# A hybrid attention block: second copies of queries and keys taken from SBUF, a changed input order, and a later first division

## The chip, the cores and the metric

The kernel runs on one core of one Trainium2 chip. The metric is the device time in microseconds of that core, from three runs of the kernel before; a separate profiled execution gives the profile.

## The reference

One decoder block over 1024 positions of width 1024, in float32. The part that matters here, cut:

```python
u = rms_norm(h, norm_mix)
proj = u @ w_in                      # S5 input, q, k, v, forget logits, gates
y_ssm = gelu(s5_ssm(...));  out_a = glu(y_ssm @ w_glu)
log_f = log_sigmoid(f_logit); cum = cumsum(log_f)
s = (q @ k.T) * 64**-0.5 + cum[t] - cum[s]       # 8 heads of 64, causal
att = softmax(s) @ v
h = h + (gate_a * out_a + gate_b * (att @ w_fox_o)) @ w_mix_out
h = h + memory_cross_attention(...)  # 256 memory tokens, 4 heads of 128, keys and values = rms_norm(mem) @ w_mem_kv
h = h + swiglu_ffn(rms_norm(h));  out = rms_norm(h)
```

## The kernel before

A float32 product is made of three matmuls of a rounded high part and a low part each (`mm3`, lines 173 to 175: high·high, high·low, low·high). A `split` makes the two parts: a cast on ScalarE (ACT, line 183) and a subtraction on VectorE (DVE, line 184). Nearly all of the time TensorE (PE) multiplies; ACT and DVE evacuate PSUM and make high and low parts; POOL (GpSimd) makes a few low parts; SP issues the DMAs.

The stages in time: input (0 to about 60 us: memory tokens and input are normalised and transposed, the keys and values of the memory and the S5 input are projected), gates and S5 (to 300), values of the forgetting attention (to 366), its eight heads (to 560), GLU and mixing (to 740), memory attention (to 920), feed-forward (to 1538).

A scheduler places each engine's instructions by the order in which the program emits them, by their dependences and by its own cost estimates. An engine executes its instructions in that order, and each waits for its semaphores. `B.behind(x)` places what is emitted in it no earlier than behind instruction `x`.

**Input.** `stage_in` emits the steps that the table `ORDER_IN` (line 41) lists. `K0` to `K3` are the projections of the four memory heads' keys (24 matmuls of 128x256 each; the weights `whi`, `wlo` of a head are split by `W0` to `W3`, `k` evacuates), `Tn0`, `Em0` and the like transpose and evacuate halves of a memory tile, `T00` to `T71` and `E..` the same for the tiles `xt` of the input (line 237 the transposes, into the PSUM banks `misc` and `pv`; lines 183 and 184 the evacuations `uh`, `ul`), `Q` the squares for the norm, `D` and `F` loads, `V` the memory's values (banks `sc`, evacuated into `kv`), `U..` the projection of the S5 input (`mm`).

**A head.** `project(h)` returns the steps of head h's queries and keys: `load`, `split` of the weights, 16 `parts` (each one contraction tile of one half of 512 positions) into a PSUM bank `mm` of three, and two `evac`. An `evac` writes four tiles `hb` (K1, K2, Q1, Q2, two sets, used by heads in turn): ACT writes the high parts to the rows 0 to 63 of Q1 and K1 (lines 1725, 1726), DVE the low parts to one half of Q2 and K2 (1727, 1729), and ACT writes the high parts a second time to the other half (1732, 1733). Scores then take two matmuls (1793 with the gates' rows and the maxima's row, 1794 with Q2 and K2).

A head has 12 units (a query half and a key tile). For each: `scores` (two matmuls into a bank `sc` of two, on the diagonal a DVE addition of the mask, line 1796; the exponential `pf` on ACT, 1800; its high part `ph` on ACT, 1805, or for four of the units on DVE, 1802; its low part `pl` on DVE, 1806, or for those four units on POOL, 1803), and one or two units later the products with the values (1818, 1819, 1825). Between the units, `run` emits what is listed in `side[i]`: row maxima of the next head (1763 on PE into `mm`, 1765 and 1768 on DVE), `parts`, `evac` and weight splits of the head after it. `max_row` turns the maxima into a row and sends it by DMA (1781). At the end of a head `finish` makes reciprocals through DRAM (`rb`), and in the next head `divide` multiplies by them (1846, DVE, 64x1024) and splits the result (`ahi`, `alo`).

Of the kernel before, what the change touches and what calls it, by code (L numbers as in the profile page):

```python
# [13 lines left out]
AF = mybir.ActivationFunctionType  # L14
# [24 lines left out]
RSLOT_LATE = (0, 1, 2, 3, 4, 4, 5, 5, 6, 6, 7, 7)  # L39

ORDER_IN = """
Fm G0 Fn G1 D0 X10 B0 b0 Qm Qn Rm D1 Sm F1 B1 Tm0 Tm1 b1 Rn Sn Tn0 F0 D2 Em0 Tn1 En0 W0 Em1 En1 D3 F2 F3 W1 C1 Q0 Q1 K0 D4 F4 F5 K1 R0
S0 T00 T01 k0 E00 Q2 W2 D5 F6 F7 E01 S1 T10 Q3 W3 k1 K3 K2 W4 E10 W5 D6 R1 k2 T11 k3 S2 Q4 V0 S3 T30
E11 D7 D8 D9 Da Q5 T20 R2 T21 E21 E20 S4 E30 W6 Db y0 L0 W7 T40 V1 S5 E40 T31 V2 E31 W8 T41 V3 E41 W9 T50 Q6 v T51 E51
U00 Q7 R3 S6g u00 L1 T60 E50 S7g Wa T61 T70 E61 Wb U10 E60 T71 E70 E71 P0 y1 U20 u10 u20 P1 U21 U11 U30
P2 u30 U31 u11 u31 U01 u21 P3 P4 P5 u01
# [20 lines left out]
def f32(ap):  # L67
    return ap.bitcast(F32)
# [1503 lines left out]
            self.B.S.dma_start(y_d[q, i].rearrange("t (m g) c -> (t m) g c", g=8), f32(y).rearrange("p (g c) -> p g c", g=8))  # L1572


Projection = namedtuple("Projection", "load split parts evac")


class Fox:
# [111 lines left out]
    def project(self, h):  # L1690

        B = self.B
        V, A, S = B.V, B.A, B.S
        K1, K2, Q1, Q2 = self.hb[h % 2]

        def load(behind=None):
            src = lambda c: self.w_in[:, c + h * DH:c + (h + 1) * DH].rearrange("(k p) c -> p k c", p=P)
            raw = self.raw[h] = B.wpool.tile([P, RAW], F32, tag="raw", bufs=4, name="raw")[:, :D]
            rv = raw.rearrange("p (k c) -> p k c", k=8)
            with B.behind(behind):  # L1700
                S.dma_start(rv[:, :, 0:64], src(C_Q))
                return S.dma_start(rv[:, :, 64:128], src(C_K))

        def parted(behind=None):
            wh = B.wpool.tile([P, WSLOT], F32R, tag="whi", name="whi")[:, :D]
            wl = B.wpool.tile([P, WSLOT], F32R, tag="wlo", name="wlo")[:, :D]
            with B.behind(behind):
                cast = B.split(wh, wl, self.raw.pop(h))
            self.pj[h] = [t.rearrange("p (k c) -> p k c", k=8) for t in (wh, wl)]
            return cast  # L1710

        def part(hf, k):
            if k == 0:
                self.pj[h, hf] = B.bank("mm")
            wh, wl = self.pj[h]
            rh, rl = self.uT.rhs(k, hf)
            with B.behind(self.maxed if h == 1 else None):
                self.parted = B.mm3(self.pj[h, hf], wh[:, k, :], wl[:, k, :], rh, rl, k == 0, k == 7)

        def evac(hf, between=None):  # L1720
            if hf == 1 and h > 1:
                self.gate_rows(h)
            ps = self.pj.pop((h, hf))
            cs = slice(512 * hf, 512 * hf + 512)
            A.activation(Q1[0:64, cs], ps[0:64, :], AF.Copy, scale=0.125)
            copied = A.copy(K1[0:64, cs], ps[64:128, :])
            V.scalar_tensor_tensor(out=Q2[64:128, cs], in0=ps[0:64, :], scalar=0.125, in1=f32(Q1[0:64, cs]),
                                   op0=ALU.mult, op1=ALU.subtract)
            V.tensor_sub(K2[0:64, cs], ps[64:128, :], f32(K1[0:64, cs]))
            cast = between(copied) if between else None  # L1730
            with B.behind(cast):
                A.activation(Q2[0:64, cs], ps[0:64, :], AF.Copy, scale=0.125)
                A.copy(K2[64:128, cs], ps[64:128, :])
            return cast

        return Projection(load, parted, [lambda hf=hf, k=k: part(hf, k) for hf in range(2) for k in range(8)],
                          [lambda: evac(0), lambda between=None: evac(1, between)])

    def gate_rows(self, h):
        K1, K2, Q1, Q2 = self.hb[h % 2]  # L1740
# [118 lines left out]
    def run(self, y_d, yT, aT, w_glu, w_d, filler):  # L1859
        B, fp, S = self.B, self.fp, self.B.S  # L1860
        self.aT = aT
        self.prepare_v()
        for t in range(NT):
            self.values_of_v(1, t)
        self.log_forget()
        self.setup()

        def load_y(k, h):

            with B.behind(self.maxima[NH - 2] if h else self.spread[NH - 4]):  # L1870
# [22 lines left out]
        for f in pro[0].parts[:8] + pro[0].evac[:1] + pro[0].parts[8:] + pro[0].evac[1:]:  # L1893
# [12 lines left out]
        with B.behind(self.negated):  # L1906
            ready = pro[1].evac[1](pro[2].split)
        self.values_of_v(0, 4)
        pro[3].load()
        self.values_of_v(0, 5, ready)  # L1910
        with B.behind(turned):
            self.values_of_v(0, 6, ready)
        units = [(qc, kt) for qc in range(2) for kt in range(4 * qc + 4)]
        for h in range(NH):
            side = {i: [] for i in range(12)}
            late = h == NH - 2
            if late:
                for i, f in enumerate(pro[h + 1].parts[8:]):
                    side[i // 2].append(f)
                side[3].append(pro[h + 1].evac[1])  # L1920
            if h + 1 < NH:
                for i, f in enumerate(self.row_max(h + 1)):
                    side[(RSLOT_LATE if late else RSLOT)[i]].append(f)
                side[9].append(lambda: self.max_row(h + 1))
            if h + 2 < NH:
                n = 8 if h + 3 == NH else 16
                for i, f in enumerate(pro[h + 2].parts[:n]):
                    side[i if n == 8 else PSLOT[i]].append(f)
                side[9].append(pro[h + 2].evac[0])
                if n == 16:  # L1930
                    side[11].append(pro[h + 2].evac[1])
            if h + 3 < NH:
                side[9].append(lambda: pro[h + 3].split(self.exp))
            for n_ in {1: (4, 5), 2: (6,), 3: (7,)}.get(h, ()):
                side[5].append(lambda n_=n_: pro[n_].load(self.spread[h - 1]))
            if h == 0:
                side[0].append(lambda: self.values_of_v(0, 7))
            if late:
                for k in range(8):
                    side[4 + k].append(lambda k=k: load_y(k % 4, k // 4))  # L1940
            if h == NH - 1:
                for k in range(3):
                    side[6 + k].append(lambda k=k: load_att(k))
                for i, f in enumerate(filler):
                    side[i * 12 // len(filler)].append(lambda i=i, f=f: first_glu(i, f))
            for i, u in enumerate(units):
                self.scores(h, *u)
                for f in side[i]:
                    f()
                if len(self.hi_todo) > 2:  # L1950
                    self.values_hi()
                if len(self.lo_todo) > 1:
                    self.values_lo()
                if h and i == 5:
                    with B.behind(self.left):
                        self.divide(h - 1)
        while self.hi_todo:
            self.values_hi()
        while self.lo_todo:
            self.values_lo()  # L1960
        self.divide(NH - 1)
# [29 lines left out]
```

## Time and profile before

| | us |
|---|---|
| median of three runs (1538.91, 1540.33, 1540.62) | 1540.33 |
| the profiled execution | 1539.77 |
| its span, first to last instruction | 1538.1 |
| PE busy in it | 1520.7 |
| DVE busy | 1005.7 |
| ACT busy | 658.1 |
| POOL busy | 253.6 |
| PE busy in 400 to 420 us | 18.76 of 20 |
| PE busy in 920 to 1520 us | 600.00 of 600 |

PE's clock was granted at 0.999 throughout. PE is busy for 99% of the span, so the other engines' busy time decides only where PE waits for them; the idle time of PE, 17.4 us, lies in a few places.

### The profile page before, as it was taken

The page shows a single profiled execution, that of the slowest core. Times are in us where ns is not written, and L with a number is a line of the kernel's source. Part 1 is how long each engine was busy: PE and PEld are TensorE (multiplying, and loading weights), DVE is VectorE, ACT ScalarE, POOL GpSimd, SP SyncE. Part 2 cuts the span into 40 slices and gives each one's busy share as a digit, 9 for nine tenths or more (in the row PEclk, how much of TensorE's full clock was granted, in tenths as well). Part 3 has the DMA queues.
Part 4 walks back from the last instruction along what each step waited for, and adds up shares of the span by engine and source line. Part 5 has one row for each costly group of instructions (what it writes and reads, how often), then busy time and mean ns, then how long its engine had stood idle before and what let it go on. Part 6 is the DMA issues. An engine that isn't in the chain of part 4 may idle for free. (4 is left out here: it accounts for less than half of the span.)

```text
span 1538.1 us, 20434 instructions
## 1 busy us (share of the span) xinstructions
PE 1520.7 (99%) x7329; PEld 1257.7 (82%) x7329; DVE 1005.7 (65%) x1828; ACT 658.1 (43%) x1183; POOL 253.6 (16%) x341
## 2 busy tenths in 40 slices
PE   8999999999999999999999999999999999999998
PEld 7888888898777678888888888888888888888886
DVE  7936554355878867675556797777777775675555
ACT  7423334324667643232435663333333333354343
POOL 1166542100121214100102200000000000101001
PEclk9999999999999999999999999999999999999999
DMA  9634556611223746378210356555544544896542
GB/s 286 161 104 102 131 128 144 180 41 16 50 46 88 192 131 198 111 218 308 89 69 1 117 204 210 162 161 160 158 158 157 157 145 139 291 391 220 192 163 110
DMA packets 196293, 234.06 MB, mean 152 GB/s; under 512 B 35576, under 2 KB 127656, under 8 KB 195680
## 3 DMA queue, kind: packets, MB, share of 16 engines
q1 hardware_dynamic: 188704, 214.93, 47.0%
q10 hardware_dynamic: 7488, 17.83, 3.1%
q8 instruction: 57, 0.93, 0.3%
q14 instruction: 44, 0.36, 0.1%
HBM read 161.94 MB, written 72.71 MB: 153 GB/s over the span
## 5 line engine op out<-in xcount | busy, mean ns | idle before, releaser
L184 DVE TENSOR_TENSOR wlo<-raw,whi 128x1024 fp32r<-128x1024 f32 (+2 forms) x120 | 126.3, 1058 | 45.4 <-ACT whi L183 44.2
L183 ACT CAST whi<-raw 128x1024 fp32r<-128x1024 f32 (+2 forms) x120 | 108.7, 910 | 105.6 <-PE mm L174 39.1
L184 DVE TENSOR_TENSOR ol<-or,oh 128x1024 fp32r<-128x1024 f32 x73 | 90.1, 1236 | 74.0 <-ACT oh L183 71.9
L173 PE MATMUL mm<-uh,whi 128*128 128x512 f32 x344 | 136.5, 397 | 0.0
L174 PE MATMUL mm<-ul,whi 128*128 128x512 f32 x344 | 135.1, 393 | 0.0
L175 PE MATMUL mm<-uh,wlo 128*128 128x512 f32 x344 | 134.5, 391 | 0.0
L183 ACT CAST oh<-or 128x1024 fp32r<-128x1024 f32 x73 | 76.9, 1054 | 105.0 <-PE mm L1108 34.2
L997 POOL TENSOR_TENSOR g<-a,c 128x512 f32<-128x512 f32 x22 | 35.7, 1621 | 389.0 <-ACT a L996 389.0
L175 PEld LDWEIGHTS mm<-uh,wlo 128*128 128x128 f32 x344 | 64.7, 188 | 13.3 <-DVE wlo L184 0.2
L1803 POOL TENSOR_TENSOR pl<-pf,ph 128x512 fp32r<-128x512 f32 (+1 forms) x32 | 36.8, 1152 | 232.5 <-DVE ph L1802 193.3
L173 PEld LDWEIGHTS mm<-uh,whi 128*128 128x128 f32 x344 | 64.8, 188 | 11.6
L174 PEld LDWEIGHTS mm<-ul,whi 128*128 128x128 f32 x344 | 64.8, 188 | 11.0
L1800 ACT ACTIVATE pf<-sc 128x512 f32<-128x512 f32 (+1 forms) x96 | 46.4, 489 | 44.5 <-DVE sc L1796 28.3
L986 DVE SCALAR_TENSOR_TENSOR c<-c,pv 128x512 f32<-128x512 f32 x22 | 15.1, 687 | 76.5 <-ACT c L985 76.4
L211 POOL TENSOR_TENSOR r<-ms,mhalf 128x1 f32<-128x1 f32 (+1 forms) x26 | 15.7, 605 | 298.6 <-DVE ms L207 258.5
L964 PE MATMUL pv<-S3h,we 128*128 128x512 f32 x176 | 57.7, 389 | 0.0
L1806 DVE TENSOR_TENSOR pl<-pf,ph 128x512 fp32r<-128x512 f32 (+2 forms) x64 | 35.3, 553 | 10.4 <-ACT ph L1805 9.8
L1108 PE MATMUL mm<-ol,oh 128*128 128x512 f32 (+1 forms) x110 | 41.9, 381 | 0.0
L1108 PE MATMUL mm<-oh,ol 128*128 128x512 f32 (+1 forms) x110 | 41.9, 381 | 0.0
L1108 PE MATMUL mm<-oh 128*128 128x512 f32 (+1 forms) x110 | 41.9, 381 | 0.0
L173 PE MATMUL sc<-uh,whi 128*128 128x512 f32 x104 | 40.8, 392 | 0.0
L173 PE MATMUL mm<-yh,whi 128*128 128x512 f32 x104 | 40.7, 392 | 0.0
(639 smaller groups left out, 4554.2 us busy)
## 6 DMA issues: line engine op xcount, KB each, us to landing
or<-c_d SPq DMA_DIRECT2D x77, 256.0 KB
wo<-in_w_ffn_out_dram SPq DMA_DIRECT2D x22, 512.0 KB
c_d<-g SPq DMA_DIRECT2D x44, 256.0 KB
t_d<-wo SPq DMA_DIRECT2D x44, 256.0 KB
or<-t_d SPq DMA_DIRECT2D x44, 256.0 KB
rawb<-in_w_ffn_in_dram SPq DMA_DIRECT2D x20, 512.0 KB
raw<-in_w_ffn_in_dram SPq DMA_DIRECT2D x20, 512.0 KB
raw<-in_w_in_dram SPq DMA_DIRECT2D x19, 512.0 KB
```

The lines of the kernel that those rows point to most:

```text
L173: T.matmul(ps, lh, rh, start=first, stop=False)
L174: T.matmul(ps, lh, rl, start=False, stop=False)
L175: return T.matmul(ps, ll, rh, start=False, stop=last)
L183: cast = self.A.copy(hi, src)
L184: self.rest = (self.G if pool_lo else self.V).tensor_sub(lo, src, f32(hi))
L211: self.G.tensor_tensor(out=r, in0=v, in1=self.mhalf[:, 0:n], op=ALU.pow)
L964: T.matmul(ps, l_[:, k, :], r_, start=first and k == 0 and i == 0, stop=k == 3 and i == 2, skip_group_check=True)
L997: G.tensor_mul(g[:, 512:], a1, c1)
L1108: T.matmul(ps, l_[:, gi], r_[:, c0:c1], start=k == 0 and (p == NP - LAST if own else p == 0 and n in (1, 2, 7)), stop=p == NP - 1 and k == ...
L1800: self.exp = A.activation(pf[:, off:], ps[:, off:], AF.Exp)
L1803: G.tensor_sub(pl[:, off:], pf[:, off:], f32(ph[:, off:]))
L1806: self.left = V.tensor_sub(pl[:, off:], pf[:, off:], f32(ph[:, off:]))
```

## The change

It has four parts.

1. The second copies leave `evac`. A new step `double` of a projection makes them from the SBUF tiles Q1 and K1 instead of PSUM. They stand behind an exponential in the head that comes just before: half 0 in `side[4]` and half 1 in `side[8]` of head h − 1; head 0's own follow its `evac` steps.
2. Between the first head's row maxima and its scores, the split of head 2's weights stood in the midst of head 1's `evac(1)`; it now follows it.
3. The first `divide`, of head 0 in head 1, stands behind unit 7 instead of 5. The other heads keep 5.
4. In `ORDER_IN`, `Em1` comes directly behind `Em0`, and `K2` ahead of `K3`.

```diff
-...Tn0 F0 D2 Em0 Tn1 En0 W0 Em1 En1 D3 ...
+...Tn0 F0 D2 Em0 Em1 Tn1 En0 W0 En1 D3 ...
-...W3 k1 K3 K2 W4...
+...W3 k1 K2 K3 W4...

-        def evac(hf, between=None):
+        def evac(hf):
...
-            cast = between(copied) if between else None
-            with B.behind(cast):
-                A.activation(Q2[0:64, cs], ps[0:64, :], AF.Copy, scale=0.125)
-                A.copy(K2[64:128, cs], ps[64:128, :])
-            return cast
+            return copied
+
+        def double(hf):
+            cs = slice(512 * hf, 512 * hf + 512)
+            with B.behind(self.exp if h else None):
+                A.copy(Q2[0:64, cs], f32(Q1[0:64, cs]))
+                A.copy(K2[64:128, cs], f32(K1[0:64, cs]))
...
-            ready = pro[1].evac[1](pro[2].split)
+            copied = pro[1].evac[1]()
+        ready = pro[2].split(copied)
...
+                side[4].append(pro[h + 1].double[0])
+                side[8].append(pro[h + 1].double[1])
...
-                if h and i == 5:
+                if h and i == (7 if h == 1 else 5):
```

Lines of the changed kernel are three higher than before from 1735 on (four in `run`'s start, six in its loop).

**The order on PE in the input**, around 20 us. The names: `mm_272` is the bank of the second head's keys, `mm_355` and `mm_380` those of the next two; `whi_328` and `wlo_329` are the third head's weights, `whi_349` the fourth's; `misc_306` and `pv_311` are transposes of an input tile. Before:

```order
L175 MATMUL mm_272<-mh1_0_111,wlo_233 128x256
L173 MATMUL mm_355<-mh0_0_110,whi_349 128x256
L174 MATMUL mm_355<-ml0_0_112,whi_349 128x256
L237 MATMUL misc_306<-ident_69,xt_205 128x128 x4
L237 MATMUL pv_311<-ident_69,xt_205 128x128 x4
L173 MATMUL mm_380<-mh0_0_110,whi_328 128x256
L174 MATMUL mm_380<-ml0_0_112,whi_328 128x256
```

Now:

```order
L173 MATMUL mm_355<-mh0_0_110,whi_328 128x256
L174 MATMUL mm_355<-ml0_0_112,whi_328 128x256
L175 MATMUL mm_355<-mh0_0_110,wlo_329 128x256
L173 MATMUL mm_355<-mh0_0_110,whi_328 128x256
L174 MATMUL mm_355<-ml0_0_112,whi_328 128x256
L175 MATMUL mm_355<-mh0_0_110,wlo_329 128x256
L173 MATMUL mm_355<-mh0_0_110,whi_328 128x256
L174 MATMUL mm_355<-ml0_0_112,whi_328 128x256
L175 MATMUL mm_355<-mh0_0_110,wlo_329 128x256
L173 MATMUL mm_355<-mh0_0_110,whi_328 128x256
L174 MATMUL mm_355<-ml0_0_112,whi_328 128x256
L237 MATMUL misc_306<-ident_69,xt_205 128x128 x4
```

The third head's matmuls now come before the fourth's, and eleven of them stand ahead of the transposes in place of two.

**The order on DVE in the input**, around 41 to 44 us, where the S5 input's first matmuls read `ul0` (the low half of a transposed input tile, `ul0_0_95`) and `wlo_578`; `kv` are the memory's values. Before:

```order
L184 TENSOR_TENSOR ul0_0_95<-misc_472,uh0_0_87 128x2x128
L209 TENSOR_SCALAR ms2_652<-ss2_611 128x2
L184 TENSOR_TENSOR ul3_0_101<-pv_556,uh3_0_93 128x2x128
L215 TENSOR_TENSOR rt2_654<-r02_653 128x2
L216 SCALAR_TENSOR_TENSOR rt2_654<-rt2_654,ms2_652 128x2
L217 SCALAR_TENSOR_TENSOR r02_653<-rt2_654,r02_653 128x2
L184 TENSOR_TENSOR wlo_578<-xw_465,whi_577 128x1024
L184 TENSOR_TENSOR ul1_0_97<-misc_472,uh1_0_89 128x2x128
L184 TENSOR_TENSOR kv_319<-sc_439,kv_318 128x512
```

Now:

```order
L184 TENSOR_TENSOR kv_319<-sc_439,kv_318 128x512
L184 TENSOR_TENSOR ul3_0_101<-pv_556,uh3_0_93 128x2x128
L215 TENSOR_TENSOR rt2_654<-r02_653 128x2
L216 SCALAR_TENSOR_TENSOR rt2_654<-rt2_654,ms2_652 128x2
L184 TENSOR_TENSOR wlo_578<-xw_465,whi_577 128x1024
L184 TENSOR_TENSOR ul0_0_95<-misc_472,uh0_0_87 128x2x128
L184 TENSOR_TENSOR kv_319<-sc_446,kv_318 128x512
L184 TENSOR_TENSOR ul1_0_97<-misc_472,uh1_0_89 128x2x128
```

`ul0` moved from ahead of `wlo_578` to behind it, and one eviction `kv` to ahead of it.

**The order on DVE in head 1**, around 408 to 416 us, where `num<-num,rb` is the division's multiply and `alo` its low part. Before:

```order
L1802 CAST ph<-pf 128x512
L1846 TENSOR_TENSOR num<-num,rb 64x1024
L1768 TENSOR_REDUCE mc<-mm 128x1
L1727 SCALAR_TENSOR_TENSOR hb_3274<-mm,hb_3273 64x512
L184 TENSOR_TENSOR alo<-num,ahi 64x1024
L1806 TENSOR_TENSOR pl<-pf,ph 128x512
L1765 ISA junk,mc<-mm,tri 128x384
```

Now:

```order
L1805 CAST ph<-pf 128x512
L1771 TENSOR_REDUCE mc<-mm 128x1
L1727 SCALAR_TENSOR_TENSOR hb_3274<-mm,hb_3273 64x512
L1809 TENSOR_TENSOR pl<-pf,ph 128x512
L1768 ISA junk,mc<-mm,tri 128x384
L1768 ISA mc 128x1
L1849 TENSOR_TENSOR num<-num,rb 64x1024
L1799 TENSOR_TENSOR sc<-sc,trk 128x128
L1771 TENSOR_REDUCE mc<-mm 128x1
L1799 TENSOR_TENSOR sc<-sc,trk 128x128
L184 TENSOR_TENSOR alo<-num,ahi 64x1024
L1805 CAST ph<-pf 128x512
```

The multiply moved behind a row maximum, a low part of head 2's projection, a subtraction and another maximum; the low part `alo` now stands ahead of a `ph` cast.

More of the change, by code (lines that the diff above doesn't have):

```diff
@@ L41 @@
 ORDER_IN = """
-Fm G0 Fn G1 D0 X10 B0 b0 Qm Qn Rm D1 Sm F1 B1 Tm0 Tm1 b1 Rn Sn Tn0 F0 D2 Em0 Tn1 En0 W0 Em1 En1 D3 F2 F3 W1 C1 Q0 Q1 K0 D4 F4 F5 K1 R0
-S0 T00 T01 k0 E00 Q2 W2 D5 F6 F7 E01 S1 T10 Q3 W3 k1 K3 K2 W4 E10 W5 D6 R1 k2 T11 k3 S2 Q4 V0 S3 T30
+Fm G0 Fn G1 D0 X10 B0 b0 Qm Qn Rm D1 Sm F1 B1 Tm0 Tm1 b1 Rn Sn Tn0 F0 D2 Em0 Em1 Tn1 En0 W0 En1 D3 F2 F3 W1 C1 Q0 Q1 K0 D4 F4 F5 K1 R0
+S0 T00 T01 k0 E00 Q2 W2 D5 F6 F7 E01 S1 T10 Q3 W3 k1 K2 K3 W4 E10 W5 D6 R1 k2 T11 k3 S2 Q4 V0 S3 T30
 E11 D7 D8 D9 Da Q5 T20 R2 T21 E21 E20 S4 E30 W6 Db y0 L0 W7 T40 V1 S5 E40 T31 V2 E31 W8 T41 V3 E41 W9 T50 Q6 v T51 E51
@@ L1572, in store @@
             self.B.S.dma_start(y_d[q, i].rearrange("t (m g) c -> (t m) g c", g=8), f32(y).rearrange("p (g c) -> p g c", g=8))
-Projection = namedtuple("Projection", "load split parts evac")
+Projection = namedtuple("Projection", "load split parts evac double")
 class Fox:
@@ L1729, in evac @@
             V.tensor_sub(K2[0:64, cs], ps[64:128, :], f32(K1[0:64, cs]))
-            cast = between(copied) if between else None
-            with B.behind(cast):
-                A.activation(Q2[0:64, cs], ps[0:64, :], AF.Copy, scale=0.125)
-                A.copy(K2[64:128, cs], ps[64:128, :])
-            return cast
+            return copied
[4 more added lines that the diff above has]
+                A.copy(K2[64:128, cs], f32(K1[0:64, cs]))
         return Projection(load, parted, [lambda hf=hf, k=k: part(hf, k) for hf in range(2) for k in range(8)],
-                          [lambda: evac(0), lambda between=None: evac(1, between)])
+                          [lambda: evac(0), lambda: evac(1)],
+                          [lambda: double(0), lambda: double(1)])
     def gate_rows(self, h):
@@ L1892, in run @@
                             w_glu[k * P:(k + 1) * P].rearrange("(g m) c -> m g c", m=16))
-        for f in pro[0].parts[:8] + pro[0].evac[:1] + pro[0].parts[8:] + pro[0].evac[1:]:
+        for f in pro[0].parts[:8] + pro[0].evac[:1] + pro[0].parts[8:] + pro[0].evac[1:] + pro[0].double:
             f()
```

## The prediction

> **What bounds the kernel now.** I read the busy shares first, then the busy time by stretch, then what TensorE waited for, and last the timeline around each of those waits.
>
> The head of the page:
>
> ```profile
> span 1538.1 us, 20434 instructions
> ...
> PE 1520.7 (99%) x7329; PEld 1257.7 (82%) x7329; DVE 1005.7 (65%) x1828; ACT 658.1 (43%) x1183; POOL 253.6 (16%) x341
> ```
>
> TensorE (PE) is idle for 1538.1 − 1520.7 = 17.4 us in all. The change adds and removes no matmul, so only some of those 17.4 us can be won. Where they lie shows in the busy time by stretch (start:end, length, then busy us of PE, PEld, DVE, ACT, POOL with instruction counts in brackets, clock, DMA share, GB/s):
>
> ```profile
> 20.00:40.00 20.00, 18.65 (x121) 16.11 (x121) 19.25 (x38) 15.51 (x33) 1.70 (x3) 1.00 0.93 236
> 400.00:420.00 20.00, 18.76 (x91) 14.06 (x91) 16.92 (x39) 11.99 (x22) 4.60 (x4) 1.00 0.50 94
> 920.00:1520.00 600.00, 600.00 (x2647) 496.41 (x2646) 399.10 (x533) 233.05 (x336) 45.43 (x30) 1.00 0.57 187
> ```
>
> The feed-forward part is full, and the change can do nothing there. What it can reach are the 1.35 us that PE is idle in 20 to 40, and holes like the 1.24 us of 400 to 420 in the attention heads. PE's waits with their causes (engine and line waited for: us in total, times, longest):
>
> ```profile
> PE mm L1763 <- DVE mc L1768: 1.2, 1, 1.2
> PE mm L173 <- ACT whi L183: 1.1, 1, 1.1
> PE misc L237 <- DVE xt L231: 1.1, 2, 0.9
> PE sc L1793 <- ACT pf L1800: 0.7, 2, 0.5
> PE pv L1818 <- DVE ph L1802: 0.5, 1, 0.5
> PE mm L1763 <- DVE mc L1765: 0.3, 1, 0.3
> PE pv L1818 <- ACT ph L1805: 0.3, 1, 0.3
> PE mm L1763 <- ACT hb L1733: 0.3, 1, 0.3
> ```
>
> The whole that the change could win if every one of these went is 1.2 + 1.1 + 1.1 + 0.7 + 0.5 + 3 × 0.3 = 5.5 us, or 0.36% of the time. That is the ceiling. The question is how much of it stays won, because PE stands in a chain with DVE and ACT, and a stall that goes lets PE run into the next late buffer.
>
> **The start (K2 ahead of K3, Em1 early).** These are the rows around 17 to 23 us (start, length, engine, line, what, and in brackets the idle time before with its releaser):
>
> ```profile
> 17.16 1.07 ACT L183 CAST whi<-raw 128x1024 fp32r<-128x1024 f32 x1
> 18.07 0.28 PE L175 MATMUL mm<-mh,wlo 128*128 128x256 f32 x1
> 18.19 0.28 PE L173 MATMUL mm<-mh,whi 128*128 128x256 f32 x1
> 18.27 1.23 DVE L184 TENSOR_TENSOR wlo<-raw,whi 128x1024 fp32r<-128x1024 f32 x1 [0.72 <-ACT whi L183]
> 20.46 1.07 ACT L183 CAST whi<-raw 128x1024 fp32r<-128x1024 f32 x1
> 20.98 2.48 DVE L231 SCALAR_TENSOR_TENSOR xt<-xt,r,gain 128x1024 f32<-128x1024 f32 x2
> 21.58 0.39 PE L173 MATMUL mm<-mh,whi 128*128 128x256 f32 x1 [1.11 <-ACT whi L183]
> 22.32 0.66 PE L237 MATMUL misc<-ident,xt 128*128 128x128 f32 x4 [0.23 <-DVE xt L231]
> ```
>
> The cast at 17.16 is that of the third head's key weights (`whi_328`), the one at 20.46 that of the fourth's (`whi_349`); before, PE needs the second of them first. After, it needs the first, whose two parts are there at 18.23 and 19.50, so PE goes on at 21.58 − 1.11 = 20.47. The transposes behind still wait for `xt`, whose first half is there at 20.98 + 1.24 = 22.22, so they start near 22.3 as before; but 11 matmuls stand in front of them in the new order instead of 2, and 9 more at 0.12 each (18.07 to 18.19) is **1.1 us** of work done in the place of the wait.
>
> That is then given back in part. At 42 to 45 us:
>
> ```profile
> 42.29 1.22 DVE L184 TENSOR_TENSOR wlo<-xw,whi 128x1024 fp32r<-128x1024 f32 x1
> 43.43 0.42 DVE L184 TENSOR_TENSOR ul<-misc,uh 128x256 fp32r<-128x256 f32 x1
> 43.76 1.28 DVE L184 TENSOR_TENSOR kv<-sc,kv 128x512 fp32r<-128x512 f32 x2
> 43.99 0.63 PE L237 MATMUL misc<-ident,xt 128*128 128x128 f32 x4
> 44.38 0.48 PE L174 MATMUL mm<-ul,whi 128*128 128x512 f32 x1
> ```
>
> After, the low half `ul0` that the matmul of 44.38 reads is made behind the `wlo` of 42.29, no longer ahead of it, and one eviction of values (`kv`) of 1.28 / 2 = 0.64 us (two take 1.28 in the trace) stands ahead of that as well; the four transposes that stood between the two matmuls come later. PE is at this matmul 1.1 + 0.39 us (44.38 − 43.99, the transposes) earlier, at 42.9. DVE, full at 19.25 of 20 us in the stretch before, gives `ul0` at 43.43 + 0.42 = 43.85 if it doesn't run earlier itself, so PE waits up to 43.85 − 42.9 = 1.0; if DVE runs earlier by the same 1.1 less the 0.64, PE waits 0.5. I take 0.7, between the two. **Start: −1.1 + 0.7 = −0.4**; ends −1.1 (nothing given back) and +0.5 (DVE no earlier, and the 0.64 on top).
>
> **The second copies.** They are 32 before and after. From a PSUM source one took 0.59 us (first row), and the nearest SBUF-source row is the cast of 128x512 (second), against the exponential of the same shape from PSUM (third):
>
> ```profile
> L1732 ACT ACTIVATE hb<-mm 64x512 fp32r<-64x512 f32 x12 | 7.1, 592 | 7.1 <-DVE hb L1729 7.0
> L1805 ACT CAST ph<-pf 128x512 fp32r<-128x512 f32 x21 | 13.0, 621 | 0.7
> L1800 ACT ACTIVATE pf<-sc 128x512 f32<-128x512 f32 x43 | 25.6, 596 | 22.3 <-PE sc L1794 12.3 <-DVE sc L1796 9.8
> ```
>
> So a copy costs 25 ns more, 32 of them 0.8 us of ACT. [...]
>
> What they no longer do is stand in front of an exponential while waiting for DVE. The wait goes (the 7.0 us of the first row), the PSUM bank `mm` of the projection comes free when DVE's two low parts are done, about 1.2 us sooner, and the exponential of the next unit isn't behind two copies. At the change from head 0 to head 1:
>
> ```profile
> 396.08 0.59 ACT L1732 ACTIVATE hb<-mm 64x512 fp32r<-64x512 f32 x1 [1.46 <-DVE hb L1729]
> 396.69 0.58 ACT L1733 CAST hb<-mm 64x512 fp32r<-64x512 f32 x1
> 397.29 0.60 ACT L1800 ACTIVATE pf<-sc 128x512 f32<-128x512 f32 x1
> 397.94 0.39 PE L1793 MATMUL sc<-hb,hb 69*128 69x256 f32 x1 [0.50 <-ACT pf L1800]
> ```
>
> The exponential follows at the end of the second copy without a gap, and PE waits for its bank. Without the copies it can begin over 1 us sooner: **−0.5** (ends −0.5 and 0). In the late heads the same pattern stands in the table of waits: `hb` L1733 0.3, `ph` L1805 0.3, and the other `pf` wait, 0.7 − 0.5 = 0.2, together 0.8. I leave 0.2 for what the copies cost at their new places, where they sit between two exponentials: **−0.6**; ends −1.6 (the waits for `mc` L1765 and `ph` L1802 go too, 0.8) and 0.
>
> **The first division.** Around 410 us:
>
> ```profile
> 408.36 1.29 POOL L1803 TENSOR_TENSOR pl<-pf,ph 128x512 fp32r<-128x512 f32 x1 [2.80 <-DVE ph L1802]
> 408.69 2.04 DVE L1846 TENSOR_TENSOR num<-num,rb 64x1024 f32<-64x1024 f32 x1 [0.41 <-DMA rb<-rd_d]
> 410.65 0.67 DVE L1768 TENSOR_REDUCE mc<-mm 128x1 f32<-128x512 f32 x1
> 411.38 0.44 PE L1763 MATMUL mm<-hb 68*128 68x384 f32 x1 [1.24 <-DVE mc L1768]
> ...
> L1846 DVE TENSOR_TENSOR num<-num,rb x8: 1208/1214/2039, 408.7 to 581.1; 64x1024 f32<-64x1024 f32 x8
> ```
>
> The multiply waits 0.41 for the reciprocals, then takes 2.04 us where the median of the eight is 1.21 (last row), while POOL's subtraction runs; the row maximum is behind it, and PE waits 1.24 for the bank that it empties. After, the multiply stands behind that maximum, a low part, a subtraction and another maximum, so at about 411: the reciprocals are long there, POOL's operation is over at 409.65, and POOL's next waits for a `ph` that DVE's order now puts behind the division. The whole 1.24 goes. [...]
>
> In return, the multiply and the low part of the division (1.21 + 1.21 us of DVE) now stand ahead of the mask additions and the `ph` cast of the following units, for which PE waits. That it costs shows nowhere in the trace of before; the bounds are 0 (hidden) and 1.2 (one multiply in full). I take 0.4, the mean of the two largest waits for a DVE row of this kind that other heads show beside their division, 0.3 (`mc` L1765) and 0.5 (`ph` L1802). **−1.24 + 0.4 = −0.8**; ends −1.2 and 0.
>
> **Sum.** −0.4 − 0.5 − 0.6 − 0.8 = −2.3 us. The profiled execution took 1539.77 (span 1538.1 and 1.7 around it), 0.56 below the median of 1540.33. 1539.77 − 2.3 = 1537.5, and 0.56 higher as a median: **1538.0 us**, 0.15% below before. What a measurement of this kernel can tell from no change is 0.2%, 3.1 us (the three runs span 1.7), so this is most likely "the same", on the faster side.
>
> **Rivals.**
> - *More comes through.* The small waits of the late heads are one thing, the freeing of banks; with the low ends of the copies (−1.6 in place of −0.6) and a division that hides whole (−1.2 in place of −0.8), and the start as forecast, the sum is −0.4 − 0.5 − 1.6 − 1.2 = −3.7, 1536.6. For it: the `hb` L1733 row is a wait for a bank. Against: most rows name `pf`, `ph` and `mc`, not a bank. [...] Chance 0.17.
> - *It returns nearly all.* DVE decides in the start (19.25 of 20 us busy) and in head 1, and the gains turn into waits for DVE a few us later: −0.5 in total, only the handover of head 0, 1539.8. For it: DVE is the releaser in four of the eight rows. Chance 0.18.
> - *Slower: head 2 starts late.* In head 1 the division now lies ahead of the last maxima, on which the row `mr` (transposed, sent by SP) and head 2's first scores hang:
>
> ```profile
> 420.07 0.72 SPq L1781 DMA_DIRECT2D hb<-mr  x1
> 423.62 0.40 PE L1793 MATMUL sc<-hb 69*128 69x512 f32 x1
> ```
>
>   Its slack is some 423.62 − 420.07 − 0.72 = 2.8 us, without the time that the write takes to land. DVE is put back by two operations of 1.21 = 2.4, of which part is idle time now; if the landing takes over 0.4 us, the slack is gone. If the delay came through at all, then up to 2.4 + 1.2 us, and the kernel would be at −2.3 + 3.6 = +1.3; with the start's upper end (+0.5 in place of −0.4) +2.2, 1542.5. To be slower by more than 3.1 it would need late gate rows on SP too. Chance 0.05 for a slow outcome of over 0.2%, another 0.06 for 1541 to 1543.
>
> **Chances.** The forecast holds 0.54. Faster by over 0.2% is below 1537.25: most of the first rival (0.15) and the lower part of the forecast's own spread (0.13), 0.28. Slower 0.07, with 0.02 for what I have not seen. Same 0.65. The range reaches from the first rival less half of the runs' spread (1536.6 − 0.85) to the start's upper end with all else returned (1540.33 + 0.5) and as much above it: 1535.7 to 1541.7.
>
> **What would show it.** Right: the wait for `whi` at 21.6 and the one at 411.4 are gone, the multiply takes 1.2 us, the exponential at the change of heads no longer follows two copies, and a new wait for a `ul` stands near 43 us. Wrong: `double` copies in the chain of waits, a multiply of 2 us at its new place, a PE gap in front of head 2's first scores, or a start that ends no earlier at 60 us than before. Since each term is below 1.3 us, a prediction off by more than 3 would mean that the order of some engine shifted in a stage that I took as full.

## The result and the profile after

The changed kernel takes 1542.47 us (median of 21 runs, 1541.12 to 1544.82), before 1540.28 (21 runs): a ratio of 1.0016 (95% interval 1.001 to 1.0022), 2.2 us slower. The forecast was 1538.0, 2.3 us faster; the time lies 0.8 us above the range. The profiled execution took 1541.71, its span 1540.0.

What PE waited for in the changed kernel (same columns as before; lines are three to six higher):

```profile
PE misc L237 <- DVE xt L231: 1.5, 2, 0.9
PE pv L1821 <- DVE ph L1805: 0.9, 2, 0.7
PE mm L174 <- DVE ul L184: 0.8, 1, 0.8
PE mm L175 <- DVE wlo L184: 0.8, 1, 0.8
PE mm L1766 <- DVE mc L1768: 0.7, 2, 0.6
PE pv L1828 <- POOL pl L1806: 0.6, 1, 0.6
...
PE sc L1796 <- ACT pf L1803: 0.6, 1, 0.6
PE misc L1781 <- DVE mboth L1779: 0.4, 1, 0.4
```

The waits that were to go are gone (1.2 for the maximum `mc`, L1768 before, at 411; 1.1 for `whi`; 0.3 for `hb`, L1733 before), but seven of these eight rows are now waits for DVE or POOL, and four of them are new or grown (`ul`, `pl` of POOL and `mboth`, which had none before, and `wlo`, 0.2 before). Busy time by stretch (length, PE busy, clock, DMA share, GB/s), in the changed kernel:

```profile
20.00:40.00 20.00, 19.40 (x128) 1.00 0.92 243
40.00:60.00 20.00, 18.41 (x95) 1.00 0.81 185
400.00:420.00 20.00, 19.83 (x96) 1.00 0.48 89
```

0.75 us are won in 20 to 40 and 1.1 in 400 to 420, where the forecast put them. The stretch from 40 to 60 loses 1.57; before, it was full:

```profile
40.00:60.00 20.00, 19.98 (x106) 1.00 0.81 186
```

A busy PE can still lose time: in this row's stretch the matmul of 512 columns that starts at 43.51 is followed by the next only at 43.99. So I also counted what PE lost: the step from one matmul's start to the next, less the shape's usual step in the kernel before (0.227 us for 512 columns, the median of 920 to 1520, where PE is busy throughout; 0.118 for 256, the median of 8 to 60), summed over a stretch. Only differences of this count mean anything.

| PE's loss, us | 20–40 | 40–100 | 366–500 | 500–580 |
|---|---|---|---|---|
| before | 3.85 | 2.60 | 9.65 | 7.27 |
| the changed kernel | 2.63 | 4.81 | 8.71 | 9.02 |
| difference | −1.22 | +2.21 | −0.94 | +1.75 |

These sum to +1.8 of the 1.9 us by which the spans differ. The gains of the start and of the early heads are there, and each is followed by a loss of nearly twice its size.

**The start.** The changed kernel:

```profile
22.48 0.66 PE L237 MATMUL misc<-ident,xt 128*128 128x128 f32 x4 [0.60 <-DVE xt L231]
43.85 0.50 PE L174 MATMUL mm<-ul,whi 128*128 128x512 f32 x1 [0.81 <-DVE ul L184]
44.82 1.15 ACT L228 ACTIVATE xt<-xt,r 128x1024 f32<-128x1024 f32 x1 [0.62 <-DVE r L217]
46.05 4.76 POOL L229 TENSOR_TENSOR xt<-xt,gain 128x1024 f32<-128x1024 f32 x2 [4.90 <-DMA kv_d<-kv]
49.72 2.17 DVE L184 TENSOR_TENSOR wlo<-xw,whi 128x1024 fp32r<-128x1024 f32 x1 [0.52 <-ACT whi L183]
51.95 0.50 PE L175 MATMUL mm<-uh,wlo 128*128 128x512 f32 x1 [0.78 <-DVE wlo L184]
```

and the same three in the kernel before:

```profile
42.44 1.17 ACT L228 ACTIVATE xt<-xt,r 128x1024 f32<-128x1024 f32 x1
43.69 4.78 POOL L229 TENSOR_TENSOR xt<-xt,gain 128x1024 f32<-128x1024 f32 x2 [1.91 <-ACT xt L228]
48.44 1.23 DVE L184 TENSOR_TENSOR wlo<-xw,whi 128x1024 fp32r<-128x1024 f32 x1 [0.53 <-ACT whi L183]
```

The wait for `ul` is the one forecast. The wait for `wlo` was not: the last step of the third norm (L217 on DVE) fell behind `ul` and `kv`, so ACT's scaling began 2.4 us later and POOL's two gain multiplies with it (their row names a DMA, but they start 0.08 us behind the end of ACT's scaling in both kernels). POOL ran until 50.81 instead of 48.47, and DVE's next `wlo`, which started at 49.72, took 2.17 us instead of 1.23.

**The late heads.** In head 6 before, the two mask additions `sc` stand ahead of the low part `alo`, and POOL's `pl` is over when DVE's `wlo` begins:

```profile
536.82 0.48 DVE L1796 TENSOR_TENSOR sc<-sc,trk 128x128 f32<-128x128 f32 x2
537.40 1.22 DVE L184 TENSOR_TENSOR alo<-num,ahi 64x1024 fp32r<-64x1024 f32 x1
538.55 0.41 DVE L1802 CAST ph<-pf 128x512 fp32r<-128x512 f32 x1
539.04 1.29 POOL L1803 TENSOR_TENSOR pl<-pf,ph 128x512 fp32r<-128x512 f32 x1 [5.57 <-DVE mboth L1776]
541.37 1.20 DVE L184 TENSOR_TENSOR wlo<-raw,whi 128x1024 fp32r<-128x1024 f32 x1
```

In the changed kernel two row maxima in place of one stand between the division's multiply and `alo`, `alo` stands ahead of both mask additions (538.93), and an eviction of 1.19 us (`sg`, 539.40) stands ahead of the `ph` that POOL waits for (540.42):

```profile
537.78 1.22 DVE L184 TENSOR_TENSOR alo<-num,ahi 64x1024 fp32r<-64x1024 f32 x1 [0.18 <-ACT ahi L183]
539.33 0.15 DVE L1779 TENSOR_REDUCE mboth<-mc 128x8 f32<-128x16 f32 x1
539.53 0.27 PE L1781 MATMUL misc<-ident,mboth 128*8 128x128 f32 x1 [0.44 <-DVE mboth L1779]
540.93 2.58 POOL L1806 TENSOR_TENSOR pl<-pf,ph 128x512 fp32r<-128x512 f32 x1 [6.80 <-DVE ph L1805]
541.17 1.20 DVE L184 TENSOR_TENSOR wlo<-raw,whi 128x1024 fp32r<-128x1024 f32 x1
543.56 0.44 PE L1828 MATMUL pv<-pl,vhi 128*65 128x512 f32 x1 [0.63 <-POOL pl L1806]
```

PE waits for `mboth` (the maxima of the next head, put together), and then for POOL's `pl`, which took 2.58 us beside DVE's `wlo`, where it took 1.29 before.

### The profile page after: what moved, and what is told of

It is laid out like the page before. It is cut to its first block, busy times and chain, and to the rows that moved or that the text cites. A ratio compares the mean times of both kernels' runs of the same rounds, so it can differ in the third digit from the quotient of the medians.

```text
span 1540.0 us, 20442 instructions
## 1 busy us (share of the span) xinstructions
PE 1521.6 (99%) x7329; PEld 1258.3 (82%) x7329; DVE 1005.4 (65%) x1828; ACT 657.1 (43%) x1183; POOL 261.1 (17%) x341
## 5 line engine op out<-in xcount | busy, mean ns | idle before, releaser
L1252 POOL TENSOR_TENSOR sg<-sg,ga 128x512 f32<-128x512 f32 x16 | 29.7, 1879 | 72.4 <-DVE sg L1245 52.1
```

The costliest lines, as they stand in the source:

```text
L1252: self.B.G.tensor_mul(self.out[j][:, cs], self.out[j][:, cs], ga)
```

## The experiments

Times are medians of 11 runs unless said, with the median of the kernel before on the same chip and the ratio of both with its interval. Their intervals reach about 1.4 us to both sides, so that the smaller effects are read from the traces.

**1. The parts alone.** `K2` ahead of `K3` only (`k_alone`), `Em1` only (`em1_alone`):

```diff
-... k1 K3 K2 W4 ...          -... Em0 Tn1 En0 W0 Em1 En1 ...
+... k1 K2 K3 W4 ...          +... Em0 Em1 Tn1 En0 W0 En1 ...
```

> Before with only K2 ahead of K3 in the input order. Theory A (the start loses because the last step of the third normalisation, L217, falls behind other work on DVE, so POOL's two gain multiplies begin 2.4 us later and run into DVE's wlo near 49.7 us, which then takes 2.2 us instead of 1.2 and holds PE for 0.8 us; with the expected 0.8 us wait for ul at 43.9): 0.9 us slower than before, with both waits in the trace and PE idle 1.6 us in 40 to 60. Rival B (the loss lies in the heads, the second copies on ACT): 0.4 us faster than before. Rival C (Em1 causes it): no change within 0.3.

> Before with only Em1 directly behind Em0. Theory A: within 0.3 us of before; POOL's gain multiplies begin at 43.7 as before and the wlo near 48 to 50 us takes 1.2 us. Rival C (Em1 is what delays the normalisation): 0.9 us slower, with the wait for wlo. Rival B: no change.

k_alone takes 1541.18 against 1540.27, 1.0006 (0.9997 to 1.0015); PE's loss from 40 to 100 is 4.96, and a `wlo` takes 2.17 beside POOL's multiply (DVE at 50.87). em1_alone takes 1540.21, 1.0000 (0.9992 to 1.0009), with a loss of 2.70 there. So `K2` brings both waits and `Em1` neither; the time of k_alone alone would not prove its 0.9 us.

The second copies and the split only (`double_alone`: the full change without its ORDER_IN and with `i == 5`), and the division only (`divide_alone`):

```diff
-                if h and i == 5:
+                if h and i == (7 if h == 1 else 5):
```

> Before with the second copies from SBUF at units 4 and 8 and the split behind evac(1), old input order, division at unit 5. Theory A: the handover from head 0 to head 1 wins 0.6, the multiply of the first division still meets POOL (2.0 us) and the 1.2 us wait stays; in the late heads the order on DVE shifts, and POOL's low part and DVE's operations meet at other places, giving back about as much or more: 0 to 1.0 us slower. Rival B (copies from SBUF on ACT hold up the exponentials in every head): 1.5 to 2.5 us slower, spread over all heads, and the waits for pf grow in heads 2 to 4 too. The forecast on record: 1.1 us faster.

> Before with only the first division at unit 7. Theory A: the multiply takes 1.2 us, the wait of 1.24 us at 411 is gone, 0.4 comes back elsewhere: 0.8 us faster. Rival (what is won comes back in the next head, since DVE is as full as before): within 0.3 us of before.

double_alone takes 1541.86, 1.0012 (1.0003 to 1.002): 1.6 us slower, more than theory A's 0 to 1.0. In its profile PE loses 9.41 in 500 to 580 (+2.14 over before) and 7.93 in 366 to 500 (−1.72), so the heads account for 0.4 of the 1.6; rival B's loss in every head isn't there. No run separates the moved split from the copies. divide_alone takes 1542.71, 1.0015 (1.0006 to 1.0024): slower, against every expectation. The wait at 411 is gone there, but:

```profile
424.80 0.58 ACT L1733 CAST hb<-mm 64x512 fp32r<-64x512 f32 x1
425.43 0.55 PE L1763 MATMUL mm<-hb,hb 68*128 68x256 f32 x2 [0.81 <-ACT hb L1733]
...
437.25 2.01 DVE L184 TENSOR_TENSOR alo<-num,ahi 64x1024 fp32r<-64x1024 f32 x1 [0.43 <-ACT ahi L183]
439.92 0.44 PE L1763 MATMUL mm<-hb,hb 68*128 68x384 f32 x1 [0.94 <-DVE mc L1768]
452.83 0.38 PE L1793 MATMUL sc<-hb,hb 69*128 69x256 f32 x1 [0.61 <-ACT pf L1800]
```

In place of the 1.24 us PE waits 0.81, 0.94 and 0.61 between 425 and 453: for the old copies, which cost PE before only at the change from head 0 and late; for a maximum behind an `alo` of 2.01 us, which met a POOL operation of 436.90; and for an exponential. PE's loss in 366 to 500 is 1.7 over before.

**2. What repeats.** Before and double_alone once more, one profile each:

> The kernel before unchanged, for a second profile. In the profiles of double_alone and divide_alone, whose input stage is that of before, PE waits 1.0 and 1.5 us near 28.5 us for a ul that stands behind a weight load that landed late; the first profile of before has no such wait. Theory A (the loads of the input stage land up to 2 us later in some executions, whatever the kernel): the wait may be there or not, and all behind 60 us is as before within 0.3 us. Rival (the changed heads' code itself makes the load late): no wait here.

> double_alone unchanged, for a second profile. Theory A: the loss from 380 to 560 is again 0.3 to 0.4 us over before (won about 1.7 us up to 500, lost 2.1 after it), while the wait near 28.4 us comes or goes. Rival: the wait near 28.4 us of about 1 us is there again, so the start belongs to the kernel.

One run each, 1540.98 and 1541.76. In before_again:

```profile
26.02 1.05 ACT L183 CAST whi<-raw 128x1024 fp32r<-128x1024 f32 x1 [2.06 <-DMA raw<-in_w_mem_kv_dram]
27.95 0.63 PE L237 MATMUL misc<-ident,xt 128*128 128x128 f32 x4 [1.33 <-DVE ul L184]
```

The late weight load comes in executions of before too (in the first profile it doesn't), so it doesn't belong to the changed heads; double_again has it once more (ACT waits 1.55 us), which alone would decide nothing. It explains up to 1.3 us between two profiles. Neither profile of the table above has it, and up to 23.5 us, ahead of it, all profiles can be compared: from 20 on PE loses 2.2 to 2.3 in all eleven with `K3` first and 1.2 in all eight with `K2` first. The heads repeat roughly: before 9.33 and 7.20 in 366 to 500 and 500 to 580, double_again 8.04 and 9.91.

**3. The start's collision.** K2 ahead of K3, and the third norm emitted earlier (`k_norm_early`); the same in the full change (`after_norm_early`):

```diff
-... T50 Q6 v T51 E51 / U00 Q7 R3 S6g u00 ...
+... T50 Q6 Q7 R3 v T51 E51 / U00 S6g u00 ...
```

> K2 ahead of K3 as in k_alone, and the third square and root of the input norm emitted earlier, so that its last step L217 stands ahead of an eviction and a low part on DVE and POOL's gain multiplies begin over 1 us sooner. Theory A (collision of POOL's multiply with DVE's wlo): the wlo near 50 us takes 1.2 to 1.4 us in place of 2.2, the wait for it (0.8 us) is gone or below 0.2, and the kernel is 0.7 us faster than k_alone, about 0.2 slower than before. Rival (the wlo is late for another reason, its cast): the wlo still ends as late and PE waits as long, k_alone's time.

> The full change, with the third square and root of the input norm emitted earlier as in k_norm_early. Theory A: the wlo near 50 us takes 1.2 to 1.6 us, the wait of 0.8 us is below 0.2, and the kernel is 0.8 to 1.2 us faster than the full change, about 1.2 slower than before, by the late heads. Rival (the start is not what slows the full change): as the full change within 0.4.

k_norm_early takes 1539.91 against 1540.5, 0.9999 (0.999 to 1.0008). The `wlo` in question:

```profile
50.28 1.59 DVE L184 TENSOR_TENSOR wlo<-xw,whi 128x1024 fp32r<-128x1024 f32 x1 [0.53 <-ACT whi L183]
```

It runs beside POOL's multiplies for 0.50 us (they end at 50.78), the one of the changed kernel for 1.09 (to 50.81), and it takes 1.59 in place of 2.17; PE's loss for it falls from 0.94 in k_alone to 0.21. So the meeting with POOL is shown as the cause of this wait. By the medians it is 1.3 under k_alone, but part of that is a chance in head 1 (below). after_norm_early takes 1541.83 against 1540.2, 1.0011 (1.0002 to 1.0019): 0.6 below the full change, less than expected and not to be told from it by the time; its PE loss from 40 to 60 is 0.7 lower.

**4. Where the copies lose.** Copies from SBUF for heads 0 to 4 or 0 to 5 only (`double_to4`, `double_to5`):

```diff
             V.tensor_sub(K2[0:64, cs], ...)
+            if h >= 5:     # 6 in double_to5
+                A.activation(Q2[0:64, cs], ps[0:64, :], AF.Copy, scale=0.125)
+                A.copy(K2[64:128, cs], ps[64:128, :])
...
+                if h + 1 < 5:
                     side[4].append(pro[h + 1].double[0])
                     side[8].append(pro[h + 1].double[1])
```

> double_alone, but only heads 0 to 4 take their second copies from SBUF; heads 5 to 7 copy from PSUM in evac as before, and DVE's order in the late heads is that of before. Theory A (the copies help in the early heads and lose in the late ones because the scheduler puts alo ahead of the mask additions and a wlo beside POOL's low part): 1.2 to 1.7 us faster in the heads than before, faster than double_alone by about 2; PE's losses after 500 us as before. Rival B (copies from SBUF cost ACT time everywhere): as double_alone to the share of heads, 0.8 slower than before.

> double_alone, but with the second copies from SBUF for heads 0 to 5 only; heads 6 and 7 copy from PSUM as before. DVE's order in head 6 is nevertheless that of double_alone: alo ahead of the two mask additions, a wlo beside POOL's low part. Theory D (the late loss of 2.1 us comes with that order on DVE): PE loses again over 0.8 us near 540 us at the transpose of the maxima, and over 1.5 us more than before from 500 to 580 in all. Rival B (it comes from the copies on ACT in heads 5 and 6): from 500 to 580 as before within 0.4.

double_to4 takes 1540.36 against 1540.5, 1.0000 (0.9991 to 1.0009). PE loses 7.17 in 500 to 580, as before, and 9.07 in 366 to 500: the late loss is gone, but the early gain is 0.3 to 0.6, not 1.2 to 1.7. double_to5 (one run, 1542.91) makes no copy from SBUF behind 491 us and still loses 9.62 in 500 to 580, and 10.18 in 366 to 500:

```profile
539.27 1.22 DVE L184 TENSOR_TENSOR alo<-num,ahi 64x1024 fp32r<-64x1024 f32 x1 [0.28 <-ACT ahi L183]
541.02 0.27 PE L1784 MATMUL misc<-ident,mboth 128*8 128x128 f32 x1 [0.92 <-DVE mboth L1782]
```

So copies on ACT in the late heads are not what loses. Between 495 and 560 us double_to4 has DVE's, ACT's and PE's orders of before, row for row, and the late loss of before. In double_to5, in the middle of head 6 (528 to 545 us), DVE's order is that of double_alone; but ACT's weight casts and PE's matmuls have moved there too. The loss goes with the order that the scheduler gives all three engines; that DVE's part of it alone would do is not shown.

The low part of that division emitted behind unit 8 (`double_alo`), and the same with the start of k_norm_early (`norm_alo`):

```diff
-                        self.divide(h - 1)
+                        self.divide(h - 1, 0 if h == 6 else None)   # 0: multiply and ahi only
+                if h == 6 and i == 8:
+                    with B.behind(self.left):
+                        self.divide(h - 1, 1)                       # alo and its DMAs
```

> double_alone, with the low part alo of the division in head 6 emitted behind unit 8, so that it stands between the two mask additions, no longer ahead of both and of the last maximum. Theory D: the wait at the transpose of the maxima near 540 us (1.0 us lost) falls below 0.5, and the kernel is 0.5 to 1.0 us faster than double_alone, that is 0.6 to 1.1 slower than before. Rival B (copies on ACT): as double_alone.

> double_alo with K2 ahead of K3 and the early third norm. Theory: the start wins 0.3 to 0.6 against before as in k_norm_early, and the heads lose 0.6 to 1.1: 0 to 0.8 slower than before. Rival (the start's gain changes nothing in the median): as double_alo.

double_alo takes 1541.85 against 1540.12, 1.0011 (1.0002 to 1.002), as double_alone. The wait for `mboth` is gone (the loss in 540 to 560 is 2.17, in double_alone 2.44), and the waits below stand in its place; in 500 to 580 PE loses 9.45, no less than before the edit:

```profile
539.15 1.21 DVE L1850 TENSOR_TENSOR alo<-num,ahi 64x1024 fp32r<-64x1024 f32 x1
539.97 0.39 PE L1796 MATMUL sc<-hb 69*128 69x256 f32 x1 [0.78 <-ACT pf L1803]
546.56 0.28 PE L1828 MATMUL pv<-pl,vhi 128*65 128x128 f32 x1 [0.42 <-DVE pl L1809]
```

norm_alo takes 1541.57, 1.0013 (1.0004 to 1.0022), 1.45 us over before where 0 to 0.8 was expected, with a loss of 8.26 in 500 to 580. Both expectations failed: the place of `alo` alone does not set the late loss. That the order of the late heads as a whole does is shown by double_to5 against double_to4; which of its rows, stays open.

**5. The first division and POOL.** One unit's low part in head 1 on DVE (`no_pool_head1`):

```diff
-        if (qc, kt) in ((0, 2), (1, 0), (1, 2), (1, 4)):
+        if (qc, kt) in ((0, 2), (1, 0), (1, 2), (1, 4)) and (h, qc, kt) != (1, 1, 2):
```

> Before, with one unit's low part in head 1 (the second query half, third key tile) made on DVE and its high part on ACT, so that no POOL operation runs while the first division's multiply does. Theory A (the multiply of 2.04 us is a multiply of 1.21 held by POOL's operation): it takes 1.21 us. Rival (it is slow for another reason, the reciprocals' DMA): 2.0 us again. DVE has 0.7 us more to do ahead of the row maximum, so the wait at 411 need not shrink much: 0.4 to 1.2.

```profile
L1846 DVE TENSOR_TENSOR num<-num,rb x8: 1208/1213/1219, 411.1 to 581.5; 64x1024 f32<-64x1024 f32 x8
```

All eight multiplies take 1.21, so it was POOL's operation that held the first. The time of its one run is 1541.89; PE still loses 1.10 at that maximum (1.41 before), since DVE has the 0.7 us to do itself. In two other kernels with the division at unit 5, k_norm_early first and best_try second:

```profile
409.34 1.21 DVE L1846 TENSOR_TENSOR num<-num,rb 64x1024 f32<-64x1024 f32 x1
409.51 2.20 POOL L1803 TENSOR_TENSOR pl<-pf,ph 128x512 fp32r<-128x512 f32 x1 [2.80 <-DVE ph L1802]
```

```profile
409.11 1.29 POOL L1809 TENSOR_TENSOR pl<-pf,ph 128x512 fp32r<-128x512 f32 x1 [2.80 <-DVE ph L1808]
409.19 2.29 DVE L1852 TENSOR_TENSOR num<-num,rb 64x1024 f32<-64x1024 f32 x1 [0.16 <-DMA rb<-rd_d]
412.13 0.44 PE L1769 MATMUL mm<-hb 68*128 68x384 f32 x1 [1.24 <-DVE mc L1774]
```

In the first the multiply starts 0.17 us ahead of POOL's operation: it goes through, POOL waits, and PE waits for nothing there. In the second it starts 0.08 us behind, and PE waits 1.24 us. Of the fourteen profiles with the division at 5 and this POOL operation, the multiply starts second in eight.

**6. Putting it together.** The copies without the move of the input (`fox_all`: the full change with the old ORDER_IN), the best parts (`best_try`: k_norm_early with double_to4), and two tries at the start's other wait: tile 2's first transposes ahead of tile 3's (`turn_swap`), and that with the early norm (`turn_norm`):

```diff
-... V0 S3 T30 ... Q5 T20 R2 ...
+... V0 T20 S3 T30 ... Q5 R2 ...
```

> The change without its input order: second copies, split and the division at unit 7, old ORDER_IN. Theory A (the change loses about 0.9 us by K2 ahead of K3 and 0.8 us in the late heads): 0.8 to 1.2 us slower than before, about 1 us faster than the full change; PE's losses from 380 to 560 as in the full change (0.8 us over before). Rival B (all of the loss is in the heads): as slow as the full change, 2.2 us.

> K2 ahead of K3 with the early third norm, second copies from SBUF for heads 0 to 4 only, division at unit 5, Em1 as before. Theory A: what k_norm_early (0.4 to 0.6 faster than before) and double_to4 (0.1 to 0.7 faster in the heads) give adds up: 0.5 to 1.3 us faster than before. Rival (each gain sets the phase in which DVE and POOL meet later, so gains do not add): within 0.4 us of before.

> Before with K2 ahead of K3, and tile 2's first transposes (T20) ahead of tile 3's (T30), so that DVE makes the low half ul0 ahead of wlo again and PE needn't wait for it at 43.9 us. The third norm's last step stands behind the next wlo, so POOL's gain multiplies start behind that wlo. Theory A (the start's loss is the wait for ul, 0.8 us, and the collision, 0.8 us; the 1.1 us of filled wait stays won): both waits gone, 1.6 us faster than k_alone, 0.5 to 1.0 faster than before, unless the late norm makes the transposes of tiles 6 and 7 wait. Rival (order is only traded): a new wait for xt or ul of over 0.5 us, and the time of before within 0.4.

> turn_swap with the third square and root emitted earlier as in k_norm_early: POOL's gain multiplies start about 1 us sooner. Theory A: no wait for ul at 43.9; POOL's multiplies run beside one or two wlo again and one of them takes 1.5 to 2.2 us; 0.2 to 1.0 faster than before. Rival: the time of before within 0.4.

fox_all takes 1541.75 against 1540.2, 1.0012 (1.0003 to 1.0021), with PE losses of 8.50 in 366 to 500 and 9.80 in 500 to 580. By the medians about 1.6 of the 2.2 us are the copies and the division and 0.6 the input order, a split within the intervals; by PE's losses it is 1.4 and 1.0. best_try takes 1540.4, 1.0004 (0.9995 to 1.0012), no gain; in its profile the multiply fell behind POOL (rows above). turn_swap takes 1543.74 against 1540.19, 1.0024 (1.0015 to 1.0033), and turn_norm 1541.87, 1.0008 (1.0000 to 1.0017); both were expected faster than before. The wait for `ul` at the matmul is gone in both, but in turn_swap

```profile
43.55 0.63 PE L237 MATMUL misc<-ident,xt 128*128 128x128 f32 x4 [0.67 <-DVE ul L184]
52.60 2.30 DVE L266 TENSOR_SCALAR edt_k<-edt_xc 128x16 f32<-128x16 f32 x1
55.50 0.44 PE L1314 MATMUL misc<-ident,craw 128*128 128x128 f32 x2 [1.57 <-DVE cT_re L1315]
```

the transposes wait for DVE's `ul` instead (its eviction frees their bank; in turn_norm these waits come to 1.7 us). A small DVE operation, which takes 0.16 us in the kernel before, takes 2.30 beside POOL's two multiplies: it ends at 54.90 and they at 54.87. None of the kernels tried beats before by more than its interval.

## Why the prediction was wrong, step by step

Counted by PE's loss in the two profiles, the start's −0.4 came out as +1.0, the handover's −0.5 as +0.2, the late heads' −0.6 as +1.75 and the division's −0.8 as −0.8; heads 2 to 4 (442 to 500 us), to which the forecast gave nothing, came out as −0.4. The moved split had no term, and no run shows its share. The steps that failed are the costs of the start and of the late heads.

- **The start, −0.4.** The won wait was right (1.11 and 0.23 gone, 0.60 left; PE's loss −1.22 in 20 to 40), and so was the new wait for `ul` (0.7 taken, 0.81 measured). The step that failed is the place where I stopped: I followed DVE's order to `ul` and not one row on, where L217 had moved, and what waits for L217 (ACT's scaling, POOL's two multiplies of 2.4 us each). Its cost was 0.8 at `wlo`, with smaller ones up to 100 us. `K2` alone measures +0.9, by an interval that includes no change.
- **Head 0 to 1, −0.5.** The exponential behind two copies is gone, as said, and 2.2 us later PE waits 0.57 for the next late buffer:

```profile
400.17 0.44 PE L1766 MATMUL mm<-hb 68*128 68x384 f32 x1 [0.57 <-DVE mc L1768]
```

  It was worth nothing: from 395 to 404 us PE loses 1.2 in the kernels with the old copies and 1.4 in those with the new. The sentence on the ceiling named this ("a stall that goes lets PE run into the next late buffer"), and the term did not apply it.
- **The late heads, −0.6.** Wrong sign: 500 to 580 loses +1.75 in the changed kernel and, over five profiles with the copies in all heads, a mean of 9.55 against 7.36 in four with the old ones. The step that failed: I costed the copies only by the waits that they leave, and never set the rows of head 6 side by side, where `alo` had changed places with the mask additions and POOL's `pl` had come beside a `wlo`. The price of the copies on ACT (618 and 608 ns now, rows below) is not it: double_to5 shows the loss with none of them there. Which of the moved rows makes it stays open.

```profile
L1736 ACT CAST hb<-hb 64x512 fp32r<-64x512 f32 x14 | 8.7, 618 | 0.2
L1735 ACT CAST hb<-hb 64x512 fp32r<-64x512 f32 x14 | 8.5, 608 | 0.0
```

  The copies' own price was well forecast: 16 and 37 ns over the PSUM source (592, 581), mean 26, against 25 taken. The 0.2 that the term left for the copies' new places was my guess, and no run shows it by itself.
- **The division, −0.8.** The size is right against the profile of before, and partly by luck. The multiply takes 1.2 and the 1.24 us wait is gone, for the reason given (POOL's operation). But it goes as well without the move, as soon as the multiply starts ahead of POOL (double_alone, 410.25 against 410.39). With the copies and the division at 5, PE loses 7.93, 8.04 and 8.12 in 366 to 500 where the multiply starts first (double_alone, double_again, norm_alo) and 9.27 where it starts second (double_alo); with the division at 7 it is 8.50 to 8.83 (fox_all, the changed kernel, after_norm_early). The move is worth 0.6 in the second case, a single profile, and costs as much in the first; alone, without the copies, it costs 2.4 by time and 1.7 by PE's loss. The term took a wait that hung on a tenth of a microsecond (0.17 us ahead of POOL in k_norm_early, 0.08 behind in best_try, there at the end of a wait of 0.16 for the reciprocals' DMA) for a property of the place. In the changed kernel the next head's multiply met POOL and started first, and PE didn't wait for POOL:

```profile
435.18 1.21 DVE L1849 TENSOR_TENSOR num<-num,rb 64x1024 f32<-64x1024 f32 x1
435.35 2.19 POOL L1806 TENSOR_TENSOR pl<-pf,ph 128x512 fp32r<-128x512 f32 x1 [2.32 <-DVE ph L1805]
```

  What the move costs, 0.6 in 418 to 442 us (a loss of 2.1 in the three profiles with the division at 7, 1.4 in the four with it at 5), lies mostly at two matmuls that take a `ph` near 428 and at one that waits for a maximum near 437, in head 2 and not in head 1, where 0.4 was put.
- **The rivals.** "It returns nearly all" had the right mechanism (DVE decides, gains become waits for DVE) and stopped at nothing returned beyond the gain. "Slower" had the right sign and the wrong place: no PE wait stands in front of head 2's first scores, and the loss lies in the input and in the late heads. That its sum of 1542.5 meets the measured 1542.47 is luck. The chance of 0.07 for slower by over 0.2% was not the fault (0.16% was measured); the range was too narrow upward, for it let three terms be worth nothing or a gain and only the start a loss.

## What to carry to other kernels

When an instruction moves in the order of an engine that others wait for, follow every row that changes places with it to the engine that waits for it, also where no wait stands in the old profile (here `L217` on DVE: ACT's scaling 2.4 us later, and a wait of 0.8 us at `wlo`), and do this in every head that the scheduler re-orders, not only in those that wait. Here each gain of PE was followed by a loss of nearly twice its size (−1.22 and +2.21, −0.94 and +1.75), so a gain below the size of the next slack was a guess of either sign; give such a gain a range that reaches as far above zero as below. A long operation whose time depends on a tenth of a microsecond's start against another engine (the multiply of 1.21 us when 0.17 ahead, of 2.29 when 0.08 behind) should be counted as a coin toss.

## What the runs showed of the hardware

In three meetings of a DVE operation of two SBUF inputs with one of POOL, the one that started second ended 1.1 us after the other, nearly its whole own time of 1.2 to 1.3 (multiply at 408.69: POOL's end at 409.65, its own at 410.73; `wlo` at 49.72: 50.81 and 51.89; POOL at 435.35: 436.39 and 437.54). In best_try and k_norm_early, too, the one that started first took its usual time (POOL 1.29, the multiply 1.21) and the other 2.29 and 2.20; but at 540.93 POOL stood 0.24 us earlier than DVE's `wlo` in the records and still ended 1.1 us after it. Even a 128x16 operation of DVE ended only with POOL's gain multiplies (L266 in turn_swap, 2.30 us to 54.90, they to 54.87; 0.16 us before). The other thing not expected is the weight load of the start: in before_again ACT waits 2.06 us for it and PE, behind that, 1.33 us for `ul`; in the first profile of the same kernel neither waits there.
